# Low parts of weights, moment sums and mean subtractions: from GpSimd to VectorE

## The chip, the cores and the metric

The kernel runs on one core of one Trainium2 chip. The metric is the device time of one execution in microseconds (us). Three runs of the kernel before took 1809.89 us in the median (1809.78 to 1812.17).

## What is computed

The reference is a small network in float32 on 512 tokens of 1024 channels. What matters here:

```
# block 1: x is (512, 1024), mem is (256, 1024)
proj = x @ w_in                    # split into xa ba ca u v xc da dg q (256 each), gate (1280)
y_a = ba * conv3(ca * xa);  y_b = u * (w_s @ layer_norm(gelu(v)) + b_s)   # spatial gating
y_c = pooled means of xc;   y_d = conv31(da * sigmoid(dg)) -> norm, silu, matmul
y_e = cross attention of q over mem
x = layer_norm(2 ** 0.25 * x + (concat(y_a..y_e) * silu(gate)) @ w_out)
# block 2, modulated by a condition vector c
x = x + g1 * mlstm(rmsnorm(x) * s1 + b1);   x = x + g2 * swiglu(rmsnorm(x) * s2 + b2)
x = x + g3 * hgrn2(rmsnorm(x) * s3 + b3);   x = x + g4 * moe(rmsnorm(x) * s4 + b4)   # 8 experts, 2 per token
out = rmsnorm(x)
```

## The kernel before

All products of activations with weights are made in two exact parts: a float32 operand is split into a high part (a rounded copy, format fp32r, made on ScalarE) and a low part (the operand less its high part), and three matmuls add up: high with high, low with high, high with low (`mm3`, L225). Weights come in chunks of at most 128 x 1024 through `wload` (L235): a DMA from SyncE's queue into `raw`, ScalarE's copy to `hi` (L250), then a subtraction to `lo`. Four chunks may be under way (pool `wsp`, 4 buffers); the `hi` of a chunk waits until TensorE has used up the chunk four before it. The subtraction stands on GpSimd (L252) or VectorE (L254), by `fast["pool"]` and the argument `pool`: on GpSimd for all chunks of block 1 after the first projection (L514, 28 of 1024 columns), for every second chunk of the output projection `w_out` (L770, 8 of 640 columns), and for the four chunks each that open the mLSTM, SwiGLU and HGRN2 parts (`cols4` with `nh`, `rows4` with `pool`).

Block 1 keeps VectorE busy beside the projections: `taps` (L521) makes the 31-tap convolution in 62 passes over 512 columns on the accumulators `ca`; the spatial gating normalizes `v` (tiles of 256 columns, L608 to L610) and leaves its products `y` (L621); the attention's `scores` and `attend` (L626, L650) use the same four PSUM banks `m` as the spatial gating. `ada` (L390) slips passes over 128 x 1024 tiles `ar` between the gates.

The block ends in a layer norm over the channels, which lie on the partitions. `p_out` (L800) makes each tile of 128 channels `x` and adds its moments to running sums a1 to a5; two of the sums, a2 and a3, are added on GpSimd by `padd` (L797). `moments` (L828) multiplies the sums with a matrix of 1/1024 (`onesk`) in halves of the tokens and works out mean `mu` (named sth in the trace), scale `rs` and the next norm's scale `rs2`. `final` (L867) subtracts the mean on GpSimd (L869), scales and shifts, and `normed` (L439) makes from it the next part's input `xh`, `xl`: for the first four tiles in halves of the tokens, then for whole tiles. The projection `m_0` of the mLSTM takes these up as they come (`cols4`, L277).

Each engine works through its own queue in a fixed order. The order is set when the program is built, by a scheduler that weighs the instructions' priorities and estimated times; the work on weights has high priority. Helpers record most operations, so L205 is any ScalarE operation, L208, L212, L213 and L216 VectorE's, L219 any matmul.

Of the kernel before, what the change touches and what calls it, by code (L numbers as in the profile page):

```python
# [8 lines left out]
F = mybir.dt.float32  # L9
# [16 lines left out]


def _consts():
# [3 lines left out]
    # [s, t]: 1 where s <= t  # L32
    c["upper"] = (i[:, None] <= i[None, :]).astype(np.float32)
    c["negmask"] = np.where(i[:, None] <= i[None, :], 0.0, -1e30).astype(np.float32)
    # pooling: 1/min(t+1, window) for the first 16 positions; windows 2,4 | 8,16
# [10 lines left out]
    # between neighbours of zero: a draw goes to the lower number  # L46
    c["thr"] = -2e-38 * c["lt"]
    # halving levels of a chunk: block of 2^(l+1); columns are the second halves' positions
# [12 lines left out]
def _cols(a, k):  # L61
    """vector of k*128 channels -> [128, k]"""
    return np.ascontiguousarray(np.asarray(a).reshape(k, 128).T)


def _cm(w, n):
    """[K, N] -> chunks [N/n, 128, K/128 * n], one contiguous run per partition"""
    K, N = w.shape
    return np.ascontiguousarray(
        w.reshape(K // 128, 128, N // n, n).transpose(2, 1, 0, 3).reshape(N // n, 128, (K // 128) * n))  # L70


def _tm(w, kk, n):
    """[K, N] -> chunks [N/n, K/(128 kk), 128, kk * n]"""
    K, N = w.shape
    return np.ascontiguousarray(
        w.reshape(K // (128 * kk), kk, 128, N // n, n).transpose(3, 0, 2, 1, 4).reshape(
            N // n, K // (128 * kk), 128, kk * n))


def _layout(inp):
    """The inputs, laid out for the chip."""
    f = {k: np.asarray(v) for k, v in inp.items()}
    cs = _consts()
    a = {}
# [41 lines left out]
    # [layer, vector, tile, channel, k]  # L127
# [26 lines left out]
    # experts: gate and up by columns 512, 512, 384 in chunks of two k; down by halves of the columns  # L154
# [20 lines left out]
def tile_kernel(ctx, tc, I, out, dbg=None, upto=99):  # L175
# [57 lines left out]
    fast = {"raw": None, "i": 0, "pool": 0}  # L233

    def wload(src, n, after=(), pool=False):  # L235
        """a chunk of weights in two exact parts"""
        fast["i"] += 1
        i = fast["i"]
        with ExitStack() as order:
# [11 lines left out]
            if pool or fast["pool"] and i % fast["pool"] == 0:  # L251
                nc.gpsimd.tensor_tensor(out=lo[:, 0:n], in0=raw[:, 0:n], in1=hi[:, 0:n].bitcast(F), op=OP.subtract)  # L252
            else:
                tt(lo[:, 0:n], raw[:, 0:n], hi[:, 0:n].bitcast(F), OP.subtract)  # L254
        return hi, lo

    def col(src, xh, xl, post, j, halves=False):
        """one tile of output channels: post(j, psum), or post(j, psum, half) for the tokens' halves"""
# [18 lines left out]
    def cols4(src, xh, xl, posts, step=2, nh=0, pre=None):  # L277
        """four tiles of output channels side by side, as the input's tiles come in
        (the first nh of them in halves of the tokens)"""
        ps = [G() for p in posts]  # L280

        def chunk(q):
            if pre is not None:
                pre(q)
            z = 512 * (q % 2)
            return wload(src[q // 2][:, z:z + 512 * step], 512 * step, (nrm["first"],) if nh and q == 6 else (), nh > 0)
# [19 lines left out]
    def rows4(src, xh, xl, post, pool=False):  # L306
        """token-major: 512 output columns of each tile of tokens"""
        ps = [G() for t in range(NT)]
        for q in range(4):
            hi, lo = wload(src[q], 1024, (nrm["first"],) if pool and q == 3 else (), pool)  # L310
# [55 lines left out]
    # [h, j, :]: one-hot in h, the first 64 columns for h = 2j, the others for 2j + 1  # L366
# [8 lines left out]
    # modulation, per channel: one tile of channels per step, between the layers' own work  # L375
# [16 lines left out]
    def ada(n, ev):  # L392
        """n steps, not before ev is there (times a one made from it)"""
# [14 lines left out]
    # mean square over the channels, as the tiles of the residual become final  # L408
# [30 lines left out]
    def normed(l, i, rs=None, before=None, nh=2):  # L439
        """rmsnorm, scaled and shifted, in two exact parts; the first nh tiles in halves of the tokens"""  # L440
# [43 lines left out]
    # ================= block 1 =================  # L484
    with ExitStack() as st:
# [14 lines left out]
        # -- conformer branch: dg, da  # L500
# [13 lines left out]
        fast["pool"] = 1  # L514
# [20 lines left out]
        # -- spatial gating: v token-major, u channel-major  # L535
# [45 lines left out]
        # -- cross attention: queries, keys, values  # L581
# [82 lines left out]
        # -- short gated conv  # L664
# [34 lines left out]
        # -- pooling  # L699
# [25 lines left out]
        # -- conformer: norm over the channels, silu, pointwise  # L725
# [24 lines left out]
        # -- gates and the output  # L750
# [19 lines left out]
        fast["pool"] = 2  # L770
        # residual, norm over the channels (about the mean of the first ones, so that the variance
        # loses nothing), and with its moments the mean square of what comes out of it
# [16 lines left out]
        # (with the means of these weights, the mean's part is in the sums)  # L789
# [3 lines left out]
        # (these take places of the next part's input until it comes)  # L793
        a5, mu, m2, s2_, s3_ = [hp.tile([128, T], F, tag=t, name="st" + t) for t in ("l6", "h6", "l5", "h7", "l7")]
        log_exp_tables()

        def padd(a, b):  # L797
            nc.gpsimd.tensor_tensor(out=a, in0=a, in1=b, op=OP.add)

        def p_out(j, ps, z=slice(0, T)):  # L800
# [13 lines left out]
            else:  # L814
# [5 lines left out]
                if j < KD - 1:  # L820
                    tt(a1, a1, xj, OP.add)
                    padd(a2, s2)
                    padd(a3, s3)
# [4 lines left out]
        def moments(h):  # L828
# [11 lines left out]
            # mean square of (x - mu) r g + b  # L840
# [26 lines left out]
        def final(k, z):  # L867
            xk = x[k][:, z]
            nc.gpsimd.tensor_tensor(out=xk, in0=xk, in1=mu[:, z], op=OP.subtract)  # L869
# [7 lines left out]
        fast["pool"] = 0  # L877
# [5 lines left out]
    # ================= layer 0: mLSTM =================  # L883
    with ExitStack() as st:
# [6 lines left out]
        # [r, h]: one-hot in h, for a row's two parts at r = h and r = 32 + h  # L891
# [3 lines left out]
        # gates, as rows: f in 0..7, i in 32..39  # L895
# [17 lines left out]
        # (the gates' rows take the places of the output's gate)  # L913
# [7 lines left out]
        def p_g(gps):  # L921
# [8 lines left out]
            # log sigmoid(f) = min(f, 0) - log(1 + exp(-|f|))  # L930
# [13 lines left out]
            for c in range(NT):  # L944
# [6 lines left out]
                # k's weight for the state: exp(u - g_last) / 8  # L951
# [23 lines left out]
        # rows between the two parts stay zero  # L975
# [3 lines left out]
        # q, k: projection, causal convolution, silu  # L979
        cols4(I["m_0"], xh, xl,  # L980
              [(lambda ps, j=j: p_qk(j, ps)) for j in range(3)] + [p_g], nh=4)
        fast["pool"] = 0
        for j in range(3, 8):
            col(I["m_qk"][j - 3], xh, xl, p_qk, j)
        # v: token-major, with a column of ones for the normalizer
        # (results take the places of chunks that are done)
# [11 lines left out]
        def p_o(j, ps):  # L998
            # sigmoid(o) = exp(-log(1 + exp(-o))), with the tables of the rest
# [5 lines left out]
        fast["pool"] = 0  # L1005
# [4 lines left out]
        for c in range(NT):  # L1010
            s = slice(128 * c, 128 * c + 128)
            # scores with their decays: [s, t] per head
# [29 lines left out]
            # (heads in the order 0 2 4 6, 1 3 5 7: two of one half of the rows share a bank)  # L1042
# [25 lines left out]
            # normalizer and head norm, per token and head  # L1068
# [15 lines left out]
        fast["pool"] = 0  # L1084
# [18 lines left out]
    # ================= layer 0: SwiGLU =================  # L1103
    with ExitStack() as st:
# [30 lines left out]
        # the others take the places of the input, then their own  # L1135
# [20 lines left out]
    # rows beyond the tokens are for empty slots  # L1156
# [23 lines left out]
    # what goes with a token: its number beyond its place's row for an empty slot, in two parts, its norm's  # L1180
    # scale and its weight, in three each; every slot begins with the row for an empty one
# [15 lines left out]
    # ================= layer 1: HGRN2 =================  # L1197
    with ExitStack() as st:
# [10 lines left out]
        # lower bounds: softmax over the layers (one of them) and its running sum less the first  # L1209
# [11 lines left out]
        for n in range(2):  # L1221
            rows4(I["h_i"][n], xh, xl, lambda t, ps: act(vi[t][:, 512 * n:512 * n + 512], ps, AF.Copy),
                  pool=n == 0)
        sg, fqk, oh = {}, {}, {}
        fast["pool"] = 0

        def p_hg(j, ps, late):
            s = W()
            if late:
                # sigmoid(g) = exp(-log(1 + exp(-g)))  # L1230
# [9 lines left out]
        def p_fq(j, ps):  # L1240
# [9 lines left out]
            else:  # L1250
                # (a chunk's q, then its odd ones decayed)
# [641 lines left out]
```

## Time and profile before

| | |
|---|---|
| median of 3 runs | 1809.89 us (1809.78 to 1812.17) |
| profiled execution | span 1807.8 us from the first to the last instruction, mean granted TensorE clock 0.979 |
| TensorE busy | 1744.2 us, 96% |
| VectorE busy | 1256.8 us, 70% |
| ScalarE busy | 852.2 us, 47% |
| GpSimd busy | 232.2 us, 13% |

The page gives a span for the profiled execution and no device time of its own; the span is 2.1 us under the median of the runs, and these 2.1 us are taken to lie around it. Where a group of instructions is shown, the number after x is their count, then come their busy time, the mean duration of one in ns, and the idle time of the engine just before them with what ended it. TensorE counts as busy at either clock, so a stretch at the lower clock does not show as idle time. The chain of work that ended last covers only the last moments of this program, so what bounds the kernel is read from TensorE's idle time.

### The profile page before, as it was taken

To read this page: it belongs to the slowest core of one execution; us is meant where nothing else is said; L and a number is where in the kernel's file an instruction comes from. 1 tells how busy PE (TensorE), PEld (TensorE's weight loads), DVE (VectorE), ACT (ScalarE), POOL (GpSimd) and SP (SyncE) were. 2 spreads that over 40 slices of the span, in tenths; PEclk is the share of its full clock that TensorE was granted. 3 is DMA by queue.
4 is the path that set the end of the run, shared out by engine and by line. 5 is a ranking of instruction groups with operands and counts; after the bars stand their busy time and mean duration, and the time that the engine had idled before them with its cause. 6 is when DMAs were issued, how large, how long until landed. Compare 5 with 4: busy or idle time off the path is not lost. (4 is left out here: it accounts for less than half of the span.)

```text
span 1807.8 us, 24118 instructions
## 1 busy us (share of the span) xinstructions
PE 1744.2 (96%) x8592; PEld 1429.6 (79%) x8592; DVE 1256.8 (70%) x1992; ACT 852.2 (47%) x1324; POOL 232.2 (13%) x158
## 2 busy tenths in 40 slices
PE   8899998999999999999999999999999999999995
PEld 7767776787788888888878888787887887887884
DVE  6886989756667776533355666655689789789787
ACT  5434334844534222232243223444667567567565
POOL 4543356000010000000120000000001111011000
PEclk9999998998999999999999999999999999999998
DMA  7414731343423777533342111104879779789785
GB/s 265 134 61 144 235 115 59 102 158 126 156 95 131 259 240 242 179 96 92 95 135 93 47 59 59 59 24 158 286 253 361 227 257 357 229 263 350 227 280 226
DMA packets 95701, 313.47 MB, mean 173 GB/s; under 512 B 10772, under 2 KB 11284, under 8 KB 95576
## 3 DMA queue, kind: packets, MB, share of 16 engines
q1 hardware_dynamic: 89864, 295.88, 48.3%
q0 software_dynamic: 3408, 11.80, 2.9%
q10 hardware_dynamic: 2304, 4.20, 0.6%
q8 instruction: 69, 1.13, 0.3%
q14 instruction: 56, 0.46, 0.1%
HBM read 299.25 MB, written 12.58 MB: 172 GB/s over the span
## 5 line engine op out<-in xcount | busy, mean ns | idle before, releaser
L205 ACT ACTIVATE hi<-raw 128x1024 fp32r<-128x1024 f32 (+3 forms) x481 | 477.6, 995 | 571.2 <-PE g L219 445.3
L216 DVE TENSOR_TENSOR lo<-raw,hi 128x1024 fp32r<-128x1024 f32 (+3 forms) x433 | 502.8, 1173 | 261.0 <-ACT hi L205 254.4
L219 PE MATMUL g<-xh,hi 128*128 128x512 f32 (+1 forms) x912 | 357.9, 394 | 8.1 <-ACT hi L205 5.8
L219 PE MATMUL g<-xl,hi 128*128 128x512 f32 (+1 forms) x912 | 358.3, 393 | 2.9 <-DVE xl L208 2.7
L219 PE MATMUL g<-xh,lo 128*128 128x512 f32 (+1 forms) x912 | 357.2, 392 | 0.0
L252 POOL TENSOR_TENSOR lo<-raw,hi 128x1024 fp32r<-128x1024 f32 (+1 forms) x48 | 123.9, 2588 | 672.4 <-ACT hi L205 666.2
L219 PEld LDWEIGHTS g<-xh,hi 128*128 128x128 f32 x912 | 173.8, 191 | 43.0 <-ACT hi L205 5.8
L219 PEld LDWEIGHTS g<-xl,hi 128*128 128x128 f32 x912 | 174.3, 191 | 39.4 <-DVE xl L208 4.7
L219 PEld LDWEIGHTS g<-xh,lo 128*128 128x128 f32 x912 | 174.0, 191 | 33.5 <-issue 1.0
L219 PE MATMUL g<-lo,eh 128*128 128x512 f32 (+1 forms) x480 | 181.3, 378 | 5.0 <-DVE lo L216 5.0
L219 PE MATMUL g<-hi,eh 128*128 128x512 f32 (+1 forms) x480 | 180.5, 377 | 0.0
L219 PE MATMUL g<-hi,el 128*128 128x512 f32 (+1 forms) x480 | 167.2, 379 | 0.0
L381 DVE SCALAR_TENSOR_TENSOR ar<-ar,one,crow 128x1024 f32<-128x1024 f32 x96 | 127.1, 1337 | 22.3 <-DMA ar<-in_ada_dram 21.0
L219 PEld LDWEIGHTS g<-lo,eh 128*128 128x128 f32 x480 | 90.7, 189 | 20.3 <-DVE lo L216 6.2
L219 PE MATMUL g<-hi,th 128*128 128x512 f32 x264 | 105.0, 398 | 0.2
L219 PE MATMUL g<-lo,th 128*128 128x512 f32 x264 | 103.7, 393 | 0.0
L219 PEld LDWEIGHTS g<-hi,eh 128*128 128x128 f32 x480 | 90.7, 189 | 14.1
L219 PEld LDWEIGHTS g<-hi,el 128*128 128x128 f32 x480 | 90.0, 189 | 13.5
L219 PE MATMUL g<-fh,hi 128*128 128x512 f32 (+1 forms) x198 | 73.1, 369 | 0.0
L219 PE MATMUL g<-fl,hi 128*128 128x512 f32 (+1 forms) x198 | 72.7, 367 | 0.0
L219 PE MATMUL g<-fh,lo 128*128 128x512 f32 (+1 forms) x198 | 72.7, 367 | 0.0
L219 PE MATMUL g<-hi,tl 128*128 128x512 f32 x176 | 69.3, 395 | 0.0
(468 smaller groups left out, 2717.8 us busy)
## 6 DMA issues: line engine op xcount, KB each, us to landing
raw<-in_e_a_dram SPq DMA_DIRECT2D x128, 512.0 KB, 5.1
ar<-in_ada_dram SPq DMA_DIRECT2D x96, 512.0 KB, 4.2
raw<-in_e_d_dram SPq DMA_DIRECT2D x80, 512.0 KB, 5.3
raw<-in_e_b_dram SPq DMA_DIRECT2D x64, 384.0 KB, 6.2
raw<-in_f_gu_dram SPq DMA_DIRECT2D x44, 512.0 KB, 3.4
raw<-in_w_in_dram SPq DMA_DIRECT2D x22, 512.0 KB, 3.4
raw<-in_f_d_dram SPq DMA_DIRECT2D x16, 512.0 KB, 3.5
raw<-in_h_fq_dram SPq DMA_DIRECT2D x16, 512.0 KB, 3.3
```

What stands on the lines that cost most here:

```text
L205: return nc.scalar.activation(out=o, in_=i, func=f, **kw).ins
L216: return nc.vector.tensor_tensor(out=o, in0=a, in1=b, op=op).ins
L219: nc.tensor.matmul(o, l, r, start=start, stop=stop)
L252: nc.gpsimd.tensor_tensor(out=lo[:, 0:n], in0=raw[:, 0:n], in1=hi[:, 0:n].bitcast(F), op=OP.subtract)
L381: nc.vector.scalar_tensor_tensor(out=raw, in0=raw, scalar=pace["one"], in1=crow, op0=OP.mult, op1=OP.mult, accum_out=mods[:, l, i, j:j + 1])
```

## The change

All that GpSimd did with two operands in SBUF in the places above goes to VectorE: the low parts (L252), the sums of moments (L798) and the subtractions of the mean (L869). The code of `fast["pool"]` and the arguments `pool` go. Comments are removed too, so line numbers after the change are lower by up to 14. The work that GpSimd does in the mixture of experts (L1565) and its fills, small copies and DMA issues stay.

```
 def wload(src, n, after=()):
...
             act(hi[:, 0:n], raw[:, 0:n], AF.Copy)
-            if pool or fast["pool"] and i % fast["pool"] == 0:
-                nc.gpsimd.tensor_tensor(out=lo[:, 0:n], in0=raw[:, 0:n], in1=hi[:, 0:n].bitcast(F), op=OP.subtract)
-            else:
-                tt(lo[:, 0:n], raw[:, 0:n], hi[:, 0:n].bitcast(F), OP.subtract)
+            tt(lo[:, 0:n], raw[:, 0:n], hi[:, 0:n].bitcast(F), OP.subtract)
...
-        fast["pool"] = 1
...
-        fast["pool"] = 2
...
-        def padd(a, b):
-            nc.gpsimd.tensor_tensor(out=a, in0=a, in1=b, op=OP.add)
...
                 if j < KD - 1:
                     tt(a1, a1, xj, OP.add)
-                    padd(a2, s2)
-                    padd(a3, s3)
+                    tt(a2, a2, s2, OP.add)
+                    tt(a3, a3, s3, OP.add)
...
         def final(k, z):
             xk = x[k][:, z]
-            nc.gpsimd.tensor_tensor(out=xk, in0=xk, in1=mu[:, z], op=OP.subtract)
+            tt(xk, xk, mu[:, z], OP.subtract)
```

The scheduler places the new instructions in VectorE's queue. The first place is in block 1, from the last passes on `v` to the spatial gating's `y` and the scores' maxima. VectorE's queue before:

```order
L216 TENSOR_TENSOR v<-v,sgrow 128x256 x4
L213 TENSOR_SCALAR v<-v,mv,rv 128x256 x2
L216 TENSOR_TENSOR v<-v,sgrow 128x256 x4
L208 SCALAR_TENSOR_TENSOR ca<-w,vec,ca 128x512 x10
L216 TENSOR_TENSOR y_346<-m,x_553 128x512
L216 TENSOR_TENSOR y_347<-m,x_586 128x512
L638 TENSOR_REDUCE sm<-m 128x2 x2
```

And now, at the same place:

```order
L216 TENSOR_TENSOR v<-v,sgrow 128x256 x4
L213 TENSOR_SCALAR v<-v,mv,rv 128x256
L216 TENSOR_TENSOR lo<-raw,hi 128x1024
L216 TENSOR_TENSOR v<-v,sgrow 128x256
L213 TENSOR_SCALAR v<-v,mv,rv 128x256
L216 TENSOR_TENSOR v<-v,sgrow 128x256 x3
L208 SCALAR_TENSOR_TENSOR ca<-w,vec,ca 128x512 x4
L216 TENSOR_TENSOR lo<-raw,hi 128x1024
L208 SCALAR_TENSOR_TENSOR ca<-w,vec,ca 128x512 x3
L216 TENSOR_TENSOR lo<-raw,hi 128x1024
L208 SCALAR_TENSOR_TENSOR ca<-w,vec,ca 128x512 x3
L216 TENSOR_TENSOR lo<-raw,hi 128x1024 x3
```

Six low parts of 1024 columns now stand ahead of `y_346`, the last three of them directly.

The second place is the end of `w_out`: tile 6 of the residual (`x_1839`) and the first half of tile 7 (`x_1840`); `w<-w,x_1839` is the sum a1, `w<-w` the sums a2 and a3 (on GpSimd before). VectorE's queue before:

```order
L208 SCALAR_TENSOR_TENSOR x_1839<-x_1839,g 128x512
L216 TENSOR_TENSOR x_1839<-x_1839,w 128x512
L208 SCALAR_TENSOR_TENSOR w<-x_1839,lw,w 128x512
L208 SCALAR_TENSOR_TENSOR stl_1868<-x_1839,lw,stl_1868 128x512
L216 TENSOR_TENSOR w<-w,x_1839 128x512
L208 SCALAR_TENSOR_TENSOR x_1840<-x_1840,g 128x256
L216 TENSOR_TENSOR x_1840<-x_1840,w 128x256
```

And now:

```order
L208 SCALAR_TENSOR_TENSOR x_1839<-x_1839,g 128x512
L216 TENSOR_TENSOR x_1839<-x_1839,w 128x512
L216 TENSOR_TENSOR lo<-raw,hi 128x1024
L208 SCALAR_TENSOR_TENSOR w<-x_1839,lw,w 128x512
L208 SCALAR_TENSOR_TENSOR stl_1868<-x_1839,lw,stl_1868 128x512
L216 TENSOR_TENSOR w<-w,x_1839 128x512
L216 TENSOR_TENSOR w<-w 128x512
L216 TENSOR_TENSOR lo<-raw,hi 128x1024
L216 TENSOR_TENSOR w<-w 128x512
L208 SCALAR_TENSOR_TENSOR x_1840<-x_1840,g 128x256
L216 TENSOR_TENSOR x_1840<-x_1840,w 128x256
```

Two low parts and two sums have come in between the two tiles, four instructions in all.

The third place is in `normed`, second half of the tokens, tiles 2 to 4 (`x_1835` to `x_1837`). VectorE's queue now (before, the two low parts stood elsewhere: one on GpSimd, one behind the last `xl` of this piece):

```order
L216 TENSOR_TENSOR x_1837<-x_1837,sth_1869 128x512
L216 TENSOR_TENSOR lo<-raw,hi 128x1024
L208 SCALAR_TENSOR_TENSOR sq<-x_1835,nA,w 128x256
L208 SCALAR_TENSOR_TENSOR sq<-x_1836,nA,w 128x256
L216 TENSOR_TENSOR lo<-raw,hi 128x1024
L208 SCALAR_TENSOR_TENSOR xl_2400<-sq,mods,xh_2392 128x256
L208 SCALAR_TENSOR_TENSOR xl_2401<-sq,mods,xh_2393 128x256
```

The second low part, of the first chunk after `m_0`, is now ahead of two `xl` tiles that TensorE needs. Beyond block 1, `normed` and the first chunks of SwiGLU and HGRN2 the queues are the same as before.

## Rows read from the trace of the kernel before

**Rows 1.** Stretches: length, busy us (instructions) PE, PEld, DVE, ACT, POOL; clock, DMA, GB/s.

```profile
20.00:315.00 295.00, 273.19 (x1309) 216.99 (x1309) 244.70 (x332) 124.20 (x207) 140.88 (x72) 0.95 0.41 134
84.00:90.70 6.70, 5.40 (x15) 3.98 (x16) 6.46 (x20) 3.49 (x15) 0.00 (x0) 0.50 0.17 51
270.00:315.00 45.00, 36.18 (x203) 31.51 (x202) 40.78 (x58) 21.68 (x43) 28.89 (x19) 0.85 0.15 50
```

**Rows 2.** TensorE's waits, 0 to 450 us: total us, times, longest.

```profile
PE m L219 <- DVE y L216: 5.0, 1, 5.0
PE m L219 <- DVE w L216: 3.9, 1, 3.9
PE m L219 <- ACT w L205: 3.2, 2, 2.0
...
PE m L219 <- DVE x L208: 2.1, 1, 2.1
```

**Rows 3.** TensorE's waits, 505 to 560 us (start of SwiGLU).

```profile
PE m L219 <- DVE ssq L216: 1.2, 1, 1.2
PE g L219 <- DVE xl L208: 0.8, 1, 0.8
```

**Rows 4.** TensorE's waits, 905 to 925 us (start of HGRN2).

```profile
PE g L219 <- DVE xl L208: 1.3, 1, 1.3
```

**Rows 5.** GpSimd's groups, whole span: count, busy us, mean ns, idle before.

```profile
L252 POOL TENSOR_TENSOR lo<-raw,hi 128x1024 fp32r<-128x1024 f32 x40 | 110.3, 2765 | 636.1 <-ACT hi L205 629.8 <-DMA raw<-in_h_i_dram 3.2 <-DMA raw<-in_w_in_dram 3.0
...
L798 POOL TENSOR_TENSOR w<-w 128x512 f32<-128x512 f32 x12 | 20.9, 1763 | 6.8 <-ACT w L205 6.8
...
L252 POOL TENSOR_TENSOR lo<-raw,hi 128x640 fp32r<-128x640 f32 x8 | 13.6, 1702 | 36.3 <-ACT hi L205 36.3
L869 POOL TENSOR_TENSOR x<-x,sth 128x256 f32<-128x256 f32 x8 | 6.5, 841 | 7.1 <-ACT sth L205 7.1
...
L869 POOL TENSOR_TENSOR x<-x,sth 128x512 f32<-128x512 f32 x4 | 5.7, 1454 | 0.0
```

**Rows 6.** VectorE's groups, 0 to 330 us.

```profile
L208 DVE SCALAR_TENSOR_TENSOR ca<-w,vec,ca 128x512 f32<-128x512 f32 x60 | 55.8, 1002 | 0.0
...
L216 DVE TENSOR_TENSOR v<-v,sgrow 128x256 f32<-128x256 f32 x8 | 9.5, 1245 | 0.0
...
L216 DVE TENSOR_TENSOR gl<-w,gh 128x512 fp32r<-128x512 f32 x10 | 6.9, 687 | 0.0
...
L216 DVE TENSOR_TENSOR lo<-raw,hi 128x1024 fp32r<-128x1024 f32 x4 | 4.9, 1216 | 0.0
...
L216 DVE TENSOR_TENSOR w<-w,m 128x256 f32<-128x256 f32 x4 | 1.6, 410 | 0.0
```

**Rows 7.** VectorE in order of time, 59 to 133 us: start, us, instructions.

```profile
65.77 8.05 DVE L216 TENSOR_TENSOR v<-v,sgrow 128x256 f32<-128x256 f32 x4
...
84.57 1.27 DVE L216 TENSOR_TENSOR y<-m,x 128x512 f32<-128x512 f32 x2
...
91.72 10.69 DVE L208 SCALAR_TENSOR_TENSOR ca<-w,vec,ca 128x512 f32<-128x512 f32 x16
...
115.12 17.07 DVE L208 SCALAR_TENSOR_TENSOR ca<-w,vec,ca 128x512 f32<-128x512 f32 x16
```

**Rows 8.** GpSimd in order of time, 92 to 133 us.

```profile
95.99 10.95 POOL L252 TENSOR_TENSOR lo<-raw,hi 128x1024 fp32r<-128x1024 f32 x2 [15.87 <-ACT hi L205]
...
115.38 2.73 POOL L252 TENSOR_TENSOR lo<-raw,hi 128x1024 fp32r<-128x1024 f32 x1 [8.41 <-ACT hi L205]
...
126.73 2.92 POOL L252 TENSOR_TENSOR lo<-raw,hi 128x1024 fp32r<-128x1024 f32 x1 [3.13 <-ACT hi L205]
```

**Rows 9.** VectorE in order of time, 270 to 325 us.

```profile
271.71 2.26 DVE L216 TENSOR_TENSOR x<-x,w 128x512 f32<-128x512 f32 x1
...
280.50 2.14 DVE L216 TENSOR_TENSOR x<-x,w 128x256 f32<-128x256 f32 x1
...
321.42 0.74 DVE L208 SCALAR_TENSOR_TENSOR xl<-sq,mods,xh 128x512 fp32r<-128x512 f32 x1
```

More of the change, by code (lines that the diff above doesn't have):

```diff
@@ L231, in log_exp_tables, with wload @@
         return tc.keep_in_program_order(nc.scalar.preload_act_table_set("natural_log_exp_and_others")).ins
-    fast = {"raw": None, "i": 0, "pool": 0}
-    def wload(src, n, after=(), pool=False):
+    fast = {"raw": None, "i": 0}
+    def wload(src, n, after=()):
         fast["i"] += 1
@@ L285, in chunk @@
             z = 512 * (q % 2)
-            return wload(src[q // 2][:, z:z + 512 * step], 512 * step, (nrm["first"],) if nh and q == 6 else (), nh > 0)
+            return wload(src[q // 2][:, z:z + 512 * step], 512 * step, (nrm["first"],) if nh and q == 6 else ())
         def some(q, hi, lo, s):
@@ L304, in cols4, with rows4 @@
             posts[j](ps[j])
-    def rows4(src, xh, xl, post, pool=False):
+    def rows4(src, xh, xl, post, first=False):
         ps = [G() for t in range(NT)]
         for q in range(4):
-            hi, lo = wload(src[q], 1024, (nrm["first"],) if pool and q == 3 else (), pool)
+            hi, lo = wload(src[q], 1024, (nrm["first"],) if first and q == 3 else ())
             for tk in range(8):
@@ L875, in final @@
                 act(xk, xk, AF.Identity, bias=LB[:, k:k + 1])
-        fast["pool"] = 0
         xh, xl = normed(0, 0, rs2, final, nh=4)
@@ L981, in tile_kernel @@
               [(lambda ps, j=j: p_qk(j, ps)) for j in range(3)] + [p_g], nh=4)
-        fast["pool"] = 0
         for j in range(3, 8):
@@ L1003, in p_o @@
             act(so[j], so[j], AF.Exp, scale=-1.0)
-        fast["pool"] = 0
         log_exp_tables()
@@ L1083, in tile_kernel @@
                 col(I["m_o"][j], xh, xl, p_o, j)
-        fast["pool"] = 0
         mh = [hp.tile([128, T], R, tag=f"h{k}", name=f"mh{k}") for k in range(KD)]
@@ L1222, in tile_kernel @@
             rows4(I["h_i"][n], xh, xl, lambda t, ps: act(vi[t][:, 512 * n:512 * n + 512], ps, AF.Copy),
-                  pool=n == 0)
+                  first=n == 0)
         sg, fqk, oh = {}, {}, {}
-        fast["pool"] = 0
         def p_hg(j, ps, late):
@@ L1381, in tile_kernel @@
                     gate(i)
-        fast["pool"] = 0
         A, B = norm_scale(1, 1)
```

## The prediction

> **What bounds the kernel now.** I read the table of engines first: TensorE is busy 96% of the span, so what can be won is its idle time and the time at the lower clock. The stretch view narrows this down. In block 1 and the layer norm behind it (20 to 315 us) TensorE is busy 273.2 of 295 us, so it idles 21.8 us, and its granted clock is 0.95 of full; VectorE is busy 244.7 us of the same stretch, 83% [rows 1]. The reader is to see there that VectorE has 50.3 us left, not much for the work of another engine. Then the waits of TensorE name what it waited for in its longest stops: VectorE's `y` (5.0 us, the scores of the attention behind the spatial gating), VectorE's a1 (3.9 us, the moments, named `w`), ScalarE's `w` (3.2 us in two, the attention's transposed weights) and VectorE's `x` (2.1 us, tile 0 of `w_out`) [rows 2]; at the start of SwiGLU and HGRN2 VectorE's `ssq` and `xl` (1.2, 0.8 and 1.3 us) [rows 3, 4]. Last I asked why VectorE was late there. It works without a break, but on the same instruction it spends different times: sixteen passes of `taps` took 10.69 us from 91.72 us on [rows 7], while GpSimd needed 10.95 us for two low parts, twice what it takes elsewhere; sixteen passes took 17.07 us from 115.12 us on [rows 7], while GpSimd made three low parts in 2.7 to 2.9 us each, the first at 115.38 and the last at 126.73 us [rows 8]. One of the two stands still while the other has two operands in SBUF. Four multiplications of 128 x 256 took 8.05 us [rows 7], where a subtraction of this size takes 0.41 [rows 6]. In the second case three low parts of 2.77 us (8.3 us, mean of [rows 5]) took 17.07 - 10.69 = 6.4 us from it: 0.77 of GpSimd's time.
>
> **What is added.** Durations on VectorE with two operands in SBUF: 1.22 us for 1024 columns, 0.69 for 512, 0.41 for 256 [rows 6]; for 640 I put 0.82 between them. 40 low parts of 1024 make 48.6 us, 8 of 640 make 6.6, 12 sums of 512 make 8.3, 8 subtractions of 256 and 4 of 512 make 6.0: 69.5 us on VectorE, of which 8 low parts (9.7 us) lie behind 315 us and 60 in block 1.
>
> **What is taken away.** On GpSimd 110.3 + 13.6 + 20.9 + 6.5 + 5.7 = 157 us [rows 5], which wait for nobody afterwards. What VectorE gets back is the time it stood still. Lower bound: the `taps`, 60 x (1.002 - 0.668) = 20 us with the 0.668 of the sixteen undisturbed passes, and the `v`, 8 x (1.245 - 0.41) = 7 us [rows 6, 7], together 27. Upper bound: 0.77 of 157, 121 us. VectorE is not always at work on two operands when GpSimd is, so I take the middle, about 75 us. VectorE's busy time then falls by some 5 us (bounds: 42 more, 51 less). GpSimd's time thus bought VectorE nothing in total, and what changes is when things are ready.
>
> The Trainium skill, SBUF — State Buffer, section "SBUF: two separate sides", says that VectorE and GpSimd share one pair of ports as an exclusive lock for a whole instruction, for VectorE instructions with two SBUF inputs too. By that rule alone VectorE would lose all of GpSimd's time in which it wants the pair; the upper bound above would be 157 instead of 121. The rows show 0.77 in a stretch that was all such work, and this decides.
>
> **The path, term by term.**
> (1) *The scores.* TensorE needs the banks of `y`. VectorE did `v` from 65.77 us and `y` at 84.57 us [rows 7]. In the new queue stand, from `v`'s last four multiplications on, ten passes (6.7 us) and six low parts (7.3 us; one of them among the `v`). The four multiplications shrink from 8.05 to 1.6 us, the ten passes lie in 73.8 to 84.6 us, 10.8 us, and shrink to 6.7: 10.5 us less against 7.3 more. The passes ahead of these lose their delay as well. So `y` comes at about 78 to 82 us; the last low part before it can't be earlier than its `hi`. TensorE was through with the scores it could do 5.0 us before 85.30, at about 80.3. I take the wait as gone: -5.0 (bounds 0 and -5.0). After the wait TensorE ran at 0.50 of its clock, the lower level of 1.2 GHz, and was busy 5.4 us in this stretch [rows 1]; at the higher level that is half: -2.5 (bounds 0 and -2.7).
> (2) *The second attention.* The transposed weights need places that `taps` leaves. Its last sixteen passes go from 17.07 us to 10.7 with three low parts between them (3.7): 2.7 us earlier, against 3.2 us of waits: -2.5 (bounds 0 and -3.2).
> (3) *Tile 0 of `w_out`.* A low part of 640 columns that GpSimd's delayed goes ahead of `x`; it shrinks by about 1 us of the 2.1: -1 (bounds +2, since a second low part now stands behind it, and -2.1).
> (4) *The layer norm.* From the start of tile 6's subtraction at 271.71 to the end of tile 7's at 282.64 [rows 9] are 10.9 us. Now: three times 0.69 for a subtraction and sums, one more 0.69, two low parts of 1.22, two multiply-adds of 0.74 (the last of [rows 9]), twice 0.41: 7.5 us, so -3.4. From there to the last `xl` at 322.16 [rows 9] are 39.5 us, most of it VectorE's. Twelve subtractions (6.0 us) and one low part (1.2) come in; 0.77 of GpSimd's 12.2 us [rows 5], 9.4 us, go: -2.2. What is late next: the low part ahead of two `xl` waits for a `hi` whose place TensorE frees only when it has used the first `m_0` chunk for both halves, and TensorE starts that after a pause, perhaps at the lower clock; VectorE may stand still there for 2 to 3 us, and behind it stand the `xl`. Against this the moments' matmuls no longer follow a wait of 3.9 us. I take -6 in all (bounds -2 and -9); TensorE idles 8.8 us in this stretch at a clock of 0.85 [rows 1], so there is so much to win.
> (5) *SwiGLU and HGRN2.* Of 1.2 + 0.8 + 1.3 us of waits [rows 3, 4] low parts of 1.22 in VectorE's queue leave about a quarter: -2.5 (bounds +1 and -3.3).
> (6) In the gates between 165 and 225 us VectorE gets ten low parts of 1.22 or 0.82 us, in a period of 5.6 us per gate that holds two passes over `ar`, and in `w_out` a tile gets 0.82 + 2 x 0.69 more. TensorE covers this as long as VectorE's work per period stays under TensorE's; I count 0 (bounds +4 and -2).
>
> Sum: -5 - 2.5 - 2.5 - 1 - 6 - 2.5 = -19.5 us on a profiled execution of 1807.8 us of span. The span stands 2.1 us under the median of the runs, and nothing before the first or behind the last instruction changes, so 1809.9 - 19.5, about 1790 us. Once earlier, the rest follows: behind 325 us TensorE does the same work in the same order.
>
> **Rivals.**
> (A) *VectorE becomes the bound.* If the long durations don't shrink as thought, 60 us come into a stretch where VectorE has 50.3 us left [rows 1], not all at the right time: if half is of use, 35 us longer, 1845 us; with the lower bound of 27 us returned, 60 - 27 - 25 = 8 us longer, 1818. It decides from the point where VectorE gets back less than about 35 us. For it: VectorE is at 83%, and gates and `w_out` leave little. Against: the same passes at 0.668 and at 1.07 us. Chance 0.08. The Trainium skill, Perfetto Trace Analysis, section "Optimizing Scalar/DVE Operations", would let a saturated VectorE hand work to GpSimd, though it adds that this may not help between these two; by its first half the time would be that of this rival, by the second near no change. The trace shows the second: 0.77 of GpSimd's time lost.
> (B) *The waits stay under other names*: low parts in VectorE's queue wait for `hi`, and `y` and `xl` wait behind them. Then only the first half of (4) and the clock are won and lost again: about 0 to -4 us, 1808. For it: three low parts directly ahead of `y`. Chance 0.09.
> (C) *Only the layer norm gains*, block 1 keeps its stops: -6 to -9, 1802. Chance 0.13.
> (D) *More comes back*: all terms at their good ends, 5 + 2.7 + 3.2 + 2.1 + 9 + 3.3 + 2 = 27, 1783, or a few us beyond where further stretches at the lower clock go. Chance 0.18.
>
> **Chances.** The forecast (1785 to 1798) has 0.52. With (A) left out below 1806 and half of (B), the range is 1779 to 1806. About 0.2% (3.6 us) is what a measurement of this kernel can tell from no change. Faster by more: forecast, C and D and a part of B, 0.86; within: 0.06, from B; slower: 0.08, from A.
>
> **What would show it.** Right: no wait of TensorE for `y` near 80 us and no stretch at half clock behind it; `taps` at 0.67 us throughout; tile 6 to tile 7 in under 8 us; VectorE's busy time within 20 us of 1256.8; the last `xl` of `m_0` some 15 us earlier. Wrong: VectorE without idle time from 160 to 320 us and TensorE waiting for `lo` there, or two-operand passes as long as before without GpSimd.

## The result and the profile after

The changed kernel took 1785.17 us in the median of four runs (1782.62 to 1785.57), the kernel before 1810.01 us beside it (1809.78 to 1812.17): 24.8 us less, a ratio of 0.9854 [0.983, 0.9878]; square brackets behind a ratio hold its 95% interval. The forecast was 1790 with a range of 1779 to 1806. The profiled execution has a span of 1783.2 us; 24.5 us of the difference are in the spans, so nearly all of it can be found in the two traces.

The page's table of engines for the changed kernel (busy us, share of the span, instructions):

```profile
PE 1735.9 (97%) x8592; PEld 1426.5 (80%) x8592; DVE 1234.0 (69%) x2064; ACT 855.0 (48%) x1325; POOL 76.6 (4%) x86
```

VectorE has taken over 48 low parts, 12 sums and 12 subtractions and is busy 22.8 us *less* than the 1256.8 us before. The stretches of [rows 1], with the same columns:

```profile
20.00:315.00 295.00, 287.45 (x1418) 231.44 (x1417) 242.75 (x422) 146.77 (x231) 7.14 (x22) 0.99 0.44 143
84.00:90.70 6.70, 6.70 (x31) 5.55 (x30) 6.39 (x16) 3.60 (x12) 0.00 (x0) 1.00 0.01 3
270.00:315.00 45.00, 40.10 (x209) 34.18 (x210) 36.70 (x67) 32.41 (x46) 3.39 (x14) 0.96 0.22 71
```

TensorE is busy 14.3 us more of these 295 us, at a clock of 0.99 where it was 0.95; its idle time there is 7.6 us instead of 21.8. The same window holds later work now, since everything has moved forward; but behind the scores, which end at 81.67 us, TensorE no longer runs at half clock either (second line). VectorE's groups that answer to [rows 5, 6]:

```profile
L216 DVE TENSOR_TENSOR lo<-raw,hi 128x1024 fp32r<-128x1024 f32 x40 | 48.7, 1221 | 25.1 <-ACT hi L205 24.9
L208 DVE SCALAR_TENSOR_TENSOR ca<-w,vec,ca 128x512 f32<-128x512 f32 x60 | 41.1, 752 | 0.0
L378 DVE SCALAR_TENSOR_TENSOR ar<-ar,one,crow 128x1024 f32<-128x1024 f32 x20 | 25.7, 1284 | 6.4 <-DMA ar<-in_ada_dram 5.0 <-ACT crow L205 1.1
L216 DVE TENSOR_TENSOR lo<-raw,hi 128x640 fp32r<-128x640 f32 x16 | 13.1, 821 | 0.7 <-ACT hi L205 0.7
...
L216 DVE TENSOR_TENSOR w<-w 128x512 f32<-128x512 f32 x12 | 7.9, 686 | 0.0
...
L216 DVE TENSOR_TENSOR x<-x,sth 128x256 f32<-128x256 f32 x8 | 3.3, 418 | 0.0
L216 DVE TENSOR_TENSOR v<-v,sgrow 128x256 f32<-128x256 f32 x8 | 3.0, 422 | 0.0
...
L216 DVE TENSOR_TENSOR x<-x,sth 128x512 f32<-128x512 f32 x4 | 2.7, 685 | 0.0
```

The sixty passes of `taps` went from 55.8 to 41.1 us of busy time, the eight multiplications of `v` from 9.5 to 3.0, a pass over `ar` from 1.55 to 1.28 us in the mean, and what came in took the durations that the prediction used. TensorE's waits from 0 to 450 us, for [rows 2]:

```profile
PE g L219 <- ACT hi L205: 5.6, 1, 5.6
PE g L219 <- ACT xh L205: 5.1, 3, 2.0
PE g L219 <- DVE lo L216: 2.1, 1, 2.1
PE m L219 <- DVE mods L382: 1.6, 1, 1.6
PE g L219 <- ACT x L205: 1.1, 1, 1.1
PE g L219 <- DVE xl L208: 0.7, 2, 0.5
PE m L219 <- DVE SE L208: 0.5, 2, 0.3
PE m L219 <- DVE x L208: 0.3, 1, 0.3
```

The first line is the start of the program. The waits for `y` (5.0), the sums `w` (3.9) and ScalarE's `w` (3.2) are gone, and that for `x` fell from 2.1 to 0.3. In their place stand longer waits for `xh` behind the layer norm (5.1 us, 2.3 before) and one that is new, 1.6 us for `mods` at 400 us. The 2.1 us for a low part, at 334 us now, were there before, at 359 us. Over the whole span TensorE's idle time (span less busy time) fell from 63.6 to 47.3 us; the rest of the 24.5 us is the clock: TensorE is busy 8.3 us less with the same 8592 matmuls.

Read along the program, the same events come earlier (cumulative, after less before): the end of the second scores 7.6 us, the first matmul of `w_out` 11.2, the reading of its second tile 17.1 and of its seventh 17.1, the last `xl` of `m_0` 24.4, the mLSTM core's start 24.9 and its end 21.1, the first `vi` of HGRN2 25.5, the end 24.5.

### The profile page after: what moved, and what is told of

Its sections match the earlier page's. It is cut to its first block, busy times and chain, and to the rows that moved or that the text cites. A ratio compares the mean times of both kernels' runs of the same rounds, so it can differ in the third digit from the quotient of the medians.

```text
span 1783.2 us, 24107 instructions
## 1 busy us (share of the span) xinstructions
PE 1735.9 (97%) x8592; PEld 1426.5 (80%) x8592; DVE 1234.0 (69%) x2064; ACT 855.0 (48%) x1325; POOL 76.6 (4%) x86
## 5 line engine op out<-in xcount | busy, mean ns | idle before, releaser
L216 DVE TENSOR_TENSOR lo<-raw,hi 128x1024 fp32r<-128x1024 f32 (+3 forms) x481 | 552.7, 1160 | 292.5 <-ACT hi L205 283.2
L378 DVE SCALAR_TENSOR_TENSOR ar<-ar,one,crow 128x1024 f32<-128x1024 f32 x96 | 122.0, 1283 | 22.5 <-DMA ar<-in_ada_dram 20.0
L219 PEld LDWEIGHTS g<-lo,eh 128*128 128x128 f32 x480 | 90.5, 189 | 19.8 <-DVE lo L216 5.9
L219 PEld LDWEIGHTS g<-hi,el 128*128 128x128 f32 x480 | 90.1, 189 | 13.5
L219 PE MATMUL g<-fh,hi 128*128 128x512 f32 (+1 forms) x198 | 73.1, 369 | 0.0
L219 PE MATMUL g<-lo,xh 128*128 128x512 f32 (+1 forms) x160 | 59.8, 374 | 2.1 <-DVE lo L216 2.1
```

Source lines behind the costliest of these rows:

```text
L216: return nc.vector.tensor_tensor(out=o, in0=a, in1=b, op=op).ins
L219: nc.tensor.matmul(o, l, r, start=start, stop=stop)
L378: nc.vector.scalar_tensor_tensor(out=raw, in0=raw, scalar=pace["one"], in1=crow, op0=OP.mult, op1=OP.mult, accum_out=mods[:, l, i, j:j + 1])
```

## The experiments

Two questions were put to the chip: does VectorE lose its time because GpSimd reads SBUF, or are the low parts late because GpSimd is slow; and do the places add up. The kernel before was run beside each group of experiments (1810.9 to 1811.7 us in the median, single runs from 1802.7 to 1815.6).

**1. Block 1 and `w_out` alone.** From the kernel before:

```
-        fast["pool"] = 1        +        fast["pool"] = 0      (block 1)
-        fast["pool"] = 2        +        fast["pool"] = 0      (w_out)
```

> From the kernel before; only the low parts of the first block's projections and of w_out are made on VectorE, everything else (sums of moments, mean subtractions, low parts of m_qk, h_f and h_i) stays on GpSimd. Theory (VectorE stands still while GpSimd reads two SBUF operands, so every place with such a GpSimd operation beside VectorE work pays by itself, and the places add up): the gain of the changed kernel up to the seventh tile of w_out comes back whole, about -17 us (1793), with the wait for y near 80 us gone and the distance of tile 6 to tile 7 of w_out still near 10.9 us. Rival 1 (only the layer norm's region pays): within 3 us of the kernel before. Rival 2 (the gain comes from a new order of the whole program and doesn't split): anything between, and the three partial gains do not add up to -24.8.

1796.11 us (1791.84 to 1801.13), ratio 0.992 [0.9894, 0.9947]: -15.5 us in the medians and -13.5 in the profiled spans. The reading of the seventh tile came 14.9 us earlier; no wait for `y` is left. From the start of tile 6's subtraction (256.78) to the end of the first half of tile 7's (266.99) passed 10.2 us, near the 10.9 of before. The -17 was missed by 1.5 us in the medians and 2.2 in the reading of the seventh tile. Of the 2.2, 1.3 were lost ahead of the first scores, which came 1.3 us later than in the changed kernel's profiled execution, and 0.7 in the scores, where the clock stood at half for 3.4 us from 79.0 us on, with no stop of TensorE before it.

**2. The layer norm alone.** From the kernel before:

```
-            nc.gpsimd.tensor_tensor(out=a, in0=a, in1=b, op=OP.add)
+            tt(a, a, b, OP.add)
-            nc.gpsimd.tensor_tensor(out=xk, in0=xk, in1=mu[:, z], op=OP.subtract)
+            tt(xk, xk, mu[:, z], OP.subtract)
-  ... wload(..., nh > 0)
+  ... wload(..., nh == 2)      # m_0 (nh = 4) on VectorE, the others as before
```

> From the kernel before; only the sums of moments, the mean subtractions and the four low parts of m_qk's first chunks go to VectorE; the low parts of the first block, of w_out, of h_f and of h_i stay on GpSimd. Theory: about -7 us (1803; the changed kernel gained 7.25 us between the reading of tile 6 and the mLSTM core), with the wait for y near 80 us as before and tile 6 to tile 7 near 7 us; part of it can be given back in the mLSTM core. Rival 1 (only this region pays): -20 to -25. Rival 2 (no region adds up): no more than -3.

1806.06 us (1802.81 to 1810.92), ratio 0.9977 [0.9951, 1.0002]: -5.6 us in the medians, -6.7 in the spans. The time alone does not tell that from no change; the trace does: up to tile 6 hardly anything moved (-0.6 us), and the last `xl` comes 6.8 us earlier, so this region gives 6.2 us by itself. The wait for `y` is there with 5.0 us, and tile 6 to tile 7 takes 6.9 us.

**3. The low parts that open SwiGLU and HGRN2 alone.** They are eight, four each; the expectation calls SwiGLU's weights `h_f`, in the kernel they are `f_gu_0`. From the kernel before:

```
-  ... wload(..., nh > 0)          +  ... wload(..., nh == 4)
-  ... wload(src[q], 1024, ..., pool)    +  ... wload(src[q], 1024, ...)
```

> From the kernel before; only the four low parts that the starts of SwiGLU and HGRN2 (h_f and h_i) had on GpSimd go to VectorE. Theory (each place pays by itself): the waits of TensorE of 0.8, 1.2 and 1.3 us there shrink, -2 to -3.5 us, the rest as before; with the block-1 part alone (-13.5 in the profiled execution) and the layer norm alone (-6.7) the three then add up to the -24.5 of the changed kernel within 2 us. Rival (parts depend on each other): 0, and some 4 us of the whole change remain that no part brings.

1807.33 us (1798.55 to 1811.84, twelve runs), ratio 0.9972 [0.9956, 0.9988]: -3.6 us. The waits of 1.2, 0.8 and 1.3 us [rows 3, 4] are gone; from the mLSTM's output projection to the first `vi` the trace is 3.5 us shorter, as in the changed kernel. (The profiled execution itself is 1.0 us longer than the one of before: block 1 lost 2 us and the mLSTM core 2.5 in it.) The three medians add up to -15.5 - 5.6 - 3.6 = -24.7 us, the whole change brought -24.8. That the two agree so closely is luck, as the intervals of the three (3 to 5 us either way) leave some 7 us for the sum; in the traces the three places give 14.9 + 6.2 + 3.5 = 24.6 us, the changed kernel 17.1 + 7.2 + 3.5 = 27.8, and 2.0 of the difference are those lost at the first scores of experiment 1. Each place pays without the others, so the rival that they depend on each other finds no support: it asked for 4 us that no part brings.

**4. GpSimd reads what nobody needs.** From the changed kernel, in `wload`, in block 1 alone:

```
+            if fast["idle"] is not None:
+                scr = fast["idle"]                    # 128 x 1024, float32
+                act(scr[:, 0:1], hi[:, 0:1].bitcast(F), AF.Copy)
+                nc.gpsimd.tensor_tensor(out=scr, in0=scr, in1=scr, op=OP.add)
```

> From the changed kernel; in the first block, behind each chunk's hi, ScalarE writes one column of a scratch tile, and GpSimd then adds this tile of 128x1024 to itself (two SBUF operands, nothing reads the result). The low parts stay on VectorE, so no low part waits for GpSimd. Theory (lock): most of the first block's gain is lost again, +8 to +17 us over the changed kernel (1793 to 1802), the wait for y near 80 us is back and VectorE's taps take over 0.9 us on average there. Rival (the gain comes from low parts that are ready 1.2 us behind hi on VectorE where GpSimd took 2.4 to 2.8): no more than +2 us (1785 to 1787), taps at 0.67 to 0.75.

**5. The same with a GpSimd that reads nothing.** The last line is twice `nc.gpsimd.memset(scr, 0.0)`.

> Control to the kernel with the unread GpSimd addition: the same extra write of ScalarE and the same scratch tile, but GpSimd fills it with zeros twice (no SBUF operand read) where it added. Theory (it is the two operands read, not GpSimd's being busy, the extra ScalarE write or the waits between them): within 2 us of the changed kernel (1783 to 1787), taps at 0.67 to 0.75. Rival (GpSimd's activity, its writes or the extra semaphores cost by themselves): the same +8 to +17 us as the kernel with the addition.

**6. The same with one operand.** The last line is twice `nc.gpsimd.tensor_copy(out=scr, in_=scr)`.

> Like the kernel with the unread GpSimd addition, but GpSimd copies the scratch tile onto itself twice (one SBUF operand read, one result written) where it added it to itself; the extra write of ScalarE stays. If only two SBUF operands shut VectorE out: within 2 us of the changed kernel and of the control that fills with zeros (1783 to 1789), taps 0.67 to 0.80. If any reading of SBUF by GpSimd does: 1795 to 1815, taps over 0.9 on average, the lost stretches as long as the copies.

The addition: 1809.74 us (1800.75 to 1813.59), ratio 0.9988 [0.9955, 1.002]. The zeros: 1787.72 us (1778.89 to 1789.46), ratio 0.9863 [0.9834, 0.9893]. The copies: 1808.22 us (1802.26 to 1811.82), ratio 0.9987 [0.997, 1.0003]. An addition whose result nobody reads takes the whole gain away, and twice as many instructions that only write cost nothing that can be told (2.5 us in the medians, 0.7 above the expected range, with the intervals of the ratios overlapping). The groups from 20 to 330 us, first with the addition:

```profile
L255 POOL TENSOR_TENSOR scr<-scr 128x1024 f32<-128x1024 f32 x28 | 69.3, 2474 | 114.6 <-ACT scr L205 114.6
L208 DVE SCALAR_TENSOR_TENSOR ca<-w,vec,ca 128x512 f32<-128x512 f32 x60 | 55.9, 994 | 0.0
L216 DVE TENSOR_TENSOR lo<-raw,hi 128x1024 fp32r<-128x1024 f32 x36 | 50.3, 1399 | 14.8 <-ACT hi L205 14.5
```

then with the zeros:

```profile
L208 DVE SCALAR_TENSOR_TENSOR ca<-w,vec,ca 128x512 f32<-128x512 f32 x60 | 41.2, 751 | 0.0
...
L255 POOL MEMSET scr<- 128x1024 f32 x28 | 26.8, 956 | 111.7 <-ACT scr L205 111.7
L256 POOL MEMSET scr<- 128x1024 f32 x28 | 26.8, 956 | 1.6
```

and with the copies:

```profile
L208 DVE SCALAR_TENSOR_TENSOR ca<-w,vec,ca 128x512 f32<-128x512 f32 x60 | 53.9, 960 | 0.0
L216 DVE TENSOR_TENSOR lo<-raw,hi 128x1024 fp32r<-128x1024 f32 x36 | 49.9, 1389 | 14.5 <-ACT hi L205 14.3
...
L255 POOL COPY scr<-scr 128x1024 f32<-128x1024 f32 x28 | 40.5, 1446 | 102.1 <-ACT scr L205 102.1
...
L256 POOL COPY scr<-scr 128x1024 f32<-128x1024 f32 x28 | 40.0, 1428 | 1.7
```

`taps` is back at 55.9 us with the addition (55.8 before the change) and 53.9 with the copies, and stays at 41.2 with the zeros. Here every low part is VectorE's, so the rival of late low parts on GpSimd falls. The loss is greater than expected (24.6 us over the changed kernel, where 8 to 17 stood), for a reason that the theory should have seen: VectorE's low parts are shut out as well (1399 ns where they take 1221) and stand in front of TensorE. Its waits from 20 to 240 us with the addition:

```profile
PE g L219 <- DVE lo L216: 9.3, 2, 8.9
PE g L219 <- DVE w L216: 6.8, 1, 6.8
```

No wait for `y` came back; the one for a low part, at 81.44 us and ahead of `y`, has its place. The additions could act by another path as well: ScalarE's write of the scratch column waits for GpSimd, 6.5 us in all with the addition and 0.6 with the zeros, which could make `hi` late. It did not set these two stops: the low part that TensorE waited 8.9 us for was made at 80.18 us, its `hi` was there at 68.02, and between the two VectorE was never idle; ahead of the second stop it worked without a break from 121.43 us on. The copies show that one operand is enough, where the prediction spoke of two. The Trainium skill, SBUF — State Buffer, section "Who interferes with whom", says just this: a VectorE instruction with two SBUF inputs contends with a GpSimd instruction that reads SBUF, not with one that only writes it. All three kernels agree.

**7. `w_out`'s low parts alone.** From the kernel before, only the second of the two lines of experiment 1.

> From the kernel before; only the eight low parts of w_out that GpSimd made go to VectorE, the first block's forty stay on GpSimd. Question: which edit brought the 5.9 us that the changed kernel gained between the start of w_out and the reading of its second tile, where the prediction had counted 1. Theory of the prediction (that term belongs to w_out's own low parts): the waits for gh (0.64) and gl (0.86) and most of the 2.09 us before the first tile's products go, w_out's first two tiles end 4 to 6 us nearer to its start. New theory (the last gates come late because VectorE is still working off what GpSimd held up in the first block): both waits stay at 0.6 to 1.2 us, the stretch gains 1.6 us at most, and the whole kernel 0 to 2 us (1808 to 1812 beside 1810).

1808.73 us (1799.98 to 1814.0), ratio 0.9989 [0.9971, 1.0007]: no change that can be told. In the kernel before the two waits in question were these, at 221.6 and 223.0 us, with half clock behind them (columns of the last line as in [rows 1]):

```profile
PE g L219 <- DVE gl L216: 0.9, 1, 0.9
...
PE g L219 <- ACT gh L205: 0.6, 1, 0.6
```

```profile
223.90:230.70 6.80, 4.71 (x10) 2.57 (x9) 4.01 (x5) 1.02 (x2) 1.55 (x1) 0.50 0.70 232
```

TensorE's waits from 20 to 315 us keep both in this experiment:

```profile
PE g L219 <- ACT gh L205: 1.5, 1, 1.5
PE g L219 <- DVE gl L216: 0.9, 1, 0.9
```

From the start of `w_out` to the reading of its second tile 19.8 us pass, in the kernel before 21.6, in the changed one 15.7: `w_out`'s own low parts give 1.8 us of the 5.9 (1.6 at most was expected). The two waits are gone where block 1's low parts leave GpSimd too (experiment 1 and the zeros of experiment 5 have neither), and with the addition of experiment 4, which GpSimd makes in block 1 alone, they are back:

```profile
PE g L219 <- ACT gh L205: 1.2, 1, 1.2
PE g L219 <- DVE gl L216: 1.2, 1, 1.2
```

The stretch takes 19.6 us there. So these waits belong to the gates. Between 163 and 212 us GpSimd still works 12.7 us beside VectorE here; in the gates of the changed kernel, in the second row, nothing:

```profile
163.00:212.00 49.00, 49.00 (x214) 39.67 (x213) 42.62 (x62) 17.93 (x28) 12.69 (x5) 1.00 0.67 222
```

```profile
158.00:204.00 46.00, 46.00 (x195) 36.29 (x194) 39.96 (x70) 19.38 (x31) 0.00 (x0) 1.00 0.78 247
```

**8 and 9. GpSimd's scalings in the mixture of experts.** They are what GpSimd still does with two SBUF operands behind block 1. TensorE waits there three times for a low part (1.25, 1.25 and 1.34 us) when GpSimd scales gathered rows. From the changed kernel:

```
-   nc.gpsimd.tensor_tensor(out=r, in0=r, in1=sc[:, 0:1].to_broadcast([t_[0], D]), op=OP.mult)
+   ts(r, r, sc[:, 0:1])                          # experiment 8, VectorE
+   act(r, r, AF.Copy, scale=sc[:, 0:1])          # experiment 9, ScalarE
```

> From the changed kernel; the ten scalings of gathered rows in the mixture of experts, the last GpSimd operations with two SBUF operands in that stage (2.1 us each), become a VectorE operation with a scalar for each partition. Theory: the three waits for a low part there (1.25, 1.25 and 1.34 us at 1348, 1481 and 1612) shrink to under 0.5 each and a half-clock stretch behind them can go: -2 to -4 us (1781 to 1783). Rival (the low parts are late for the transfer of the weights, not for GpSimd): the waits stay and the time is within 1 us. Rival (VectorE now waits for the gather's landing with the low parts queued behind): +1 to +3 us.

> From the changed kernel; the same ten scalings go to ScalarE instead, which reads the row with a scale for each partition. Theory: the same three waits shrink, since GpSimd reads no two operands there any more, but each scaling (about 1.06 us by the form of the hi copies of 1024) stands before hi copies in ScalarE's queue: -1 to -4 us (1781 to 1784). Rival (transfers set these waits): within 1 us. Rival (ScalarE queues behind the gather): +1 to +3 us.

1798.32 us (1793.2 to 1803.04), ratio 0.9938 [0.9916, 0.996], and 1797.78 us (1789.16 to 1801.22), ratio 0.9929 [0.9902, 0.9955]: about 13 us slower than the changed kernel. The last rival decided in both, and at four times its price. VectorE in order of time in experiment 8 (start, us; in brackets the idle time before):

```profile
1333.30 0.14 DVE L1532 TENSOR_REDUCE iw<-m 64x1 f32<-64x3 f32 x1
1340.17 0.75 DVE L212 TENSOR_SCALAR row<-row,sc 128x1024 f32<-128x1024 f32 x1 [6.73 <-DMA row<-hnd,ii]
1340.84 0.95 DVE L216 TENSOR_TENSOR lo<-raw,hi 128x768 fp32r<-128x768 f32 x1
```

VectorE stands still 6.7 us until the gathered rows land, with the low parts of the running expert queued behind, and TensorE's waits from 1285 to 1765 us become

```profile
PE g L219 <- DVE lo L216: 13.0, 3, 5.1
```

where they were 4.3, with a stretch at half clock behind each of the three. In experiment 9 ScalarE stands still for the landings (6.6, 6.4 and 4.4 us), and TensorE waits 6.5, 6.3 and 4.3 us for `eh`, which VectorE makes from ScalarE's Silu, again with half clock behind each. On GpSimd the same wait held up nobody.

**10 to 12. The scalings where the rows have landed, beside the changed kernel.** The transposes read the rows from 15 us after the first landing on. The scalings are issued behind the third block of columns of the running expert:

```
+            if after is not None:
+                with tc.issue_after(late):       # the product (VectorE) or the Silu (ScalarE) of block 3
+                    for t_ in after[0]:
+                        ts(t_[4], t_[4], t_[5][:, 0:1])                    # experiment 11
+                        act(t_[4], t_[4], AF.Copy, scale=t_[5][:, 0:1])    # experiment 12
```

> The changed kernel itself, beside the other three on one chip, so that they can be compared with it directly and not over the kernel before. Theory: about -25 us to the kernel before, as it was (ratio 0.983 to 0.988). If the first comparison had caught a lucky order of VectorE and GpSimd: ratio over 0.99.

> From the changed kernel; the ten scalings of gathered rows go to VectorE as in the kernel that was slower, but behind the product with the gated half of the third block of columns, some 10 us behind the issue, when the rows have landed (in the changed kernel they land at 1340.6 and are read by the transposes from 1355 on). Theory (GpSimd's reads delay the low parts in these places, and the loss of the first version came from low parts queued behind the gather's landing): the three waits of 1.25 to 1.34 us for a low part go under 0.5, no new wait over 1 us: -2 to -4 us beside the changed kernel. Rival (the waits of 1.25 us come from the transfers): within 1 us. Rival (the landing still is late there): +3 or more.

> The same with ScalarE: the scalings stand behind the Silu of the third block of columns. Theory: the same gain, -1 to -4 us beside the changed kernel, a little less if a hi copy has to stand behind 1.15 us of scaling. Rival (ScalarE's queue delays the next hi): +1 to +3 us.

The changed kernel again: 1783.68 us (1773.16 to 1789.0), ratio 0.9831 [0.9807, 0.9855], so the first comparison was no lucky order. Late on VectorE: 1783.14 us (1773.77 to 1786.6), 0.9835 [0.9812, 0.9858]. Late on ScalarE: 1776.42 us (1771.06 to 1782.06), 0.9808 [0.9791, 0.9825]. The experts' stretch, from the first to the last matmul of `th`, in the changed kernel (this second profiled execution) and in the one with ScalarE:

```profile
1290.50:1763.60 473.10, 467.94 (x2251) 389.60 (x2249) 391.97 (x511) 319.02 (x436) 52.95 (x29) 1.00 0.85 284
```

```profile
1282.10:1749.20 467.10, 466.77 (x2251) 389.90 (x2249) 381.02 (x511) 325.43 (x445) 31.23 (x20) 1.00 0.86 287
```

It is 6.0 us shorter, and TensorE's idle time in it falls from 5.2 to 0.3 us; with VectorE it is 469.9 us, and three waits of 0.4 to 0.9 us for `eh` are left. TensorE's waits for a low part in this stretch, 3.9 us in the changed kernel, are gone with VectorE and 0.2 us with ScalarE, so they came from GpSimd's reading and not from the transfers. The times of whole runs show no gain with VectorE (0.5 us, where 2 to 4 were expected) and put ScalarE's version 7.3 us ahead in the medians, with intervals that overlap; so the gain rests on this stretch, one profiled execution each. ScalarE's version has the lowest median of the study.

## Why the prediction was right, and where it was off

The mechanism is shown: GpSimd's reading shuts VectorE out, and the order of what is ready when changes with it. In one point it is wider than the prediction had it: one operand that GpSimd reads is enough. By the steps of the prediction:

- *What VectorE gets back.* 75 us were taken between bounds of 27 and 121. It took over 69.3 us (48.8 + 6.6 + 7.9 + 3.3 + 2.7, by the means of the groups above) and is busy 22.8 us less, so it got back about 92, and the limit of 20 us around 1256.8 was just missed. Rival (A), which needed less than 35, was far off. The lower bound was put together wrongly: it set a mean duration, 1.002 us, against 0.668, the time from one pass to the next in a row of passes that overlap a little. The passes gave back 55.8 - 41.1 = 14.7 us, not 20. And the 0.41 us of [rows 6] is a subtraction with one operand in PSUM (`m`); with both in SBUF it took 0.418, so nothing hangs on that.
- *(1) The scores.* -7.5 forecast. The wait of 5.0 us is gone, the first `y` is made at 77.75 us and the second at 79.79 (78 to 82 was said), and the second scores end 7.6 us earlier, after 0.5 us were lost at the program's start.
- *(2) The second attention.* -2.5 forecast, -3.6 measured from the second scores to the first matmul of `w_out`, a little over the end of the bounds (-3.2); the wait for ScalarE's `w` is gone whole.
- *(3) and (6) Tile 0 of `w_out`, and the gates: the step that failed.* -1 and 0 were forecast, with -2.1 and -2 as bounds; the changed kernel gained 5.9 us from the start of `w_out` to the reading of its second tile, in a second profiled execution (experiment 10) 2.6. The waits for `gh` and `gl` (1.5 us in the trace of before) had no term at all, and the half clock behind them (6.8 us of it in the trace of before) none either. With them the place adds up: 1.5 us, 1.8 of the wait for `x`, and half of the 4.7 us that TensorE was busy at half clock make 5.7 of the 5.9. The prediction put the place down to `w_out`'s own low parts; experiment 7 shows that those alone bring 1.8 us, and experiments 1 and 4 that GpSimd's reading in the first block, beside VectorE's passes over `ar` in the gates, makes the last gates late. The two executions of the changed kernel differ by the wait for `x`, 0.3 or 1.95 us, and by 3.4 us at half clock behind the longer one; from the start of `w_out` on VectorE waits 0.7 us for transfers of `ar` in the one and 1.5 in the other, which explains about half of the longer wait.
- *(4) The layer norm.* -6 forecast, -7.25 measured, -6.2 by itself (experiment 2). Tile 6 to tile 7 took 6.9 us (7.5 said). The expected stop ahead of the two `xl` is there, smaller than said (2 to 3 us):

```profile
282.86 1.23 DVE L216 TENSOR_TENSOR lo<-raw,hi 128x1024 fp32r<-128x1024 f32 x1 [1.30 <-ACT hi L205]
```

- *(5) SwiGLU and HGRN2.* -2.5 forecast, -3.5 measured.
- *Behind it.* "Once earlier, the rest follows" held but for the mLSTM core: in the profiled execution it gave 3.9 us back (73.1 us for 69.3, the granted clock at 0.84 for 0.88). In the second execution it took 69.6 us and with the late scalings on ScalarE 64.3 at a clock of 0.97, so this varies from one execution to the next, and no run puts it down to the change.

The steps measured sum to -8 - 3.6 - 5.9 - 7.25 - 3.5 = -28, less 3.9 given back. Against the forecast's -19.5, the gates and tile 0 make up 4.9 us of the difference and every other term about one each; so the time came out at the fast end of the forecast's 1785 to 1798, 2 us from rival (D), whose "further stretches at the lower clock go" is what the gates did. That it stayed within 1785 to 1798 is in part luck: without the 3.9 us given back it would have been about 1781. Rival (C) falls with experiment 1, where block 1 gains most of it, and (B) with the waits, of which none that is new or grew is over 2.1 us. The prediction's taps at "0.67 us throughout" were too strict: 0.752 in the mean, since a pass that stands by itself shows some 0.74.

## What to carry to other kernels

Work that is moved from VectorE to GpSimd to relieve VectorE may give nothing back, if it reads SBUF while VectorE works on two SBUF operands: compare the same VectorE instruction with and without GpSimd beside it, over every stretch in which GpSimd is busy, and give each of them a term, also where TensorE seems covered. Work that waits for a transfer is another matter: on an engine with nothing behind it the wait is free, and moved into a busy queue it costs the wait and everything that is queued there, unless it is put where the transfer has landed.

## What was not expected of the hardware

- One order of instructions has two outcomes. In the kernel before, VectorE's 18 passes from 35.26 us took 17.12 us; in experiments 2 and 3, whose block 1 is the same, 17.15 and 17.17. In experiment 7, where the instructions of this stretch stand in the same order, it was GpSimd that waited: 18 passes in 12.63 us, three low parts in 11.97. The passes began 1.3 us later than in the kernel before and GpSimd's low parts 2.5; what decides between the two was not tested.

```profile
36.52 12.63 DVE L208 SCALAR_TENSOR_TENSOR ca<-w,vec,ca 128x512 f32<-128x512 f32 x18
```

```profile
44.15 11.97 POOL L252 TENSOR_TENSOR lo<-raw,hi 128x1024 fp32r<-128x1024 f32 x3 [5.49 <-ACT hi L205]
```

The wait for `y`, 5.0, 5.0 and 3.5 us in the other three, was not there in that execution, and its second scores ended 5.6 us earlier than before with no edit ahead of them: one profiled execution is one draw. Whether this makes up the spread of the kernel before (1802.7 to 1815.6 us) was not tested; the changed kernel, with 7.1 us of GpSimd work left of 140.9 between 20 and 315 us, spread as much (1773.2 to 1789.0 us), and in its two traces the stretches at half clock differ.

- A VectorE instruction with one SBUF tensor and two values per partition as operands was shut out too: 1.98 us beside GpSimd's addition in experiment 4, where four of them in the changed kernel take 411 ns each.

```profile
67.73 1.98 DVE L213 TENSOR_SCALAR v<-v,mv,rv 128x256 f32<-128x256 f32 x1
```
